# Seven block products for eight in a hybrid decoder block: Strassen's scheme in the input projections, V and O turned after it, output stages moved to the end

## The chip, the cores and the metric

The kernel runs on one core of a Trainium2 chip. Times are microseconds (us) on the device from the first to the last work of one launch. The kernel before took 1591.51 us (median of 3 runs, 1591.41 to 1595.69). The profile shows one execution of it, whose span is 1588.2 us.

The engines are named as the profile names them: PE multiplies matrices, PEld loads its stationary operand, DVE does elementwise work with one or two inputs, ACT elementwise functions with one input (copies among them), POOL is a further elementwise engine, and SP issues every DMA of this kernel, in order.

## What is computed

One decoder block, in float32, on 2048 tokens of 1024 features:

```python
xn = rms_norm(x, norm_w)
proj = xn @ w_in                       # 1024 -> 5632
u_a, z_a, q_b, f_b, i_b, og_b, z_b, g_a, g_b = jnp.split(proj, SPLIT_POINTS, axis=-1)
y_a = s5_branch(u_a, z_a, ...)         # diagonal state space, GELU, GLU (512 -> 512), SiLU gate
y_b = hgrn2_branch(q_b, f_b, i_b, og_b, z_b, lower_bounds, hgrn_norm_w)   # 4 heads of 128, gated recurrence
merged = sigmoid(g_a) * (y_a @ w_proj_a) + sigmoid(g_b) * (y_b @ w_proj_b)    # 512 -> 1024 each
return rms_norm(x + merged @ w_out, final_norm_w)                          # 1024 -> 1024
```

The input projection `xn @ w_in` is by far the largest product. It is the one that the change computes in another way.

## The kernel before

**Products in pieces.** Each float32 operand of the large products is split (`split`): ACT writes a rounded copy, the high part (L94), and DVE subtracts it from the operand, the low part (L95). A product is the sum of three matmuls: high by high, low by high, high by low. So 128 by 128 weights against 512 tokens take three matmuls of 512 columns.

**Tiles.** The tokens go in two halves of 1024 (index `a`), each of two blocks of 512 (index `b`). The 5632 columns of `w_in` are 22 slices of 256: two for u, four for a head's q and f together (QF), four for a head's values and output gates (VO), two each for the SiLU gates zb and za, four each for the merge gates ga and gb. The normalised input is prepared once per half (`norm_apply`, L191: scale, then split) into 16 pairs of tiles, which stay in SBUF.

**Slices.** `proj_feat` computes a slice with features on the partitions: per block and group of 128 features 8 steps of three matmuls (L234 to L236), 96 matmuls of 512 columns in all. The VO slices go through `proj_tok`, which puts the tokens on the partitions, since the recurrence wants V and O so: 192 matmuls of 256 columns per slice (L261 to L263). ACT takes V and O out of the accumulators (L674 to L678). So 36 slices of the first kind and 8 of the second are computed, over both halves.

**What sets the order.** PE follows the program as it is written (`manual_schedule`). The generators `weave` and `mix` put the steps of the recurrence (`hgrn_core`), of the state-space scan (`ssm`) and of the small stages between the slices. A scheduler orders the other engines by its own estimate, and each of them then works strictly in its order. A half runs from its u slices to its output: projections, merge (`merge`), output product (`out_proj`); then the second half does the same. The second half's input is normalised during the first half's output product. The merge gates wait in DRAM (`sg_d`) and the branch outputs YA and YB in SBUF.

**Buffers.** PSUM has eight banks: four for the projections (`psd`), two for the recurrence's scores (`psc`), and one each in `psm` and `pss`. Weights are loaded in pieces of 512 KB, one ahead.

Of the kernel before, what the change touches and what calls it, by code (L numbers as in the profile page):

```python
# [31 lines left out]
def hybrid_block(  # L32
# [31 lines left out]
    rp = ctx.enter_context(tc.tile_pool(name="rp", bufs=32))  # L64
    wpool = ctx.enter_context(tc.tile_pool(name="wpool", bufs=3))
    yp = ctx.enter_context(tc.tile_pool(name="yp", bufs=8))
    sp = ctx.enter_context(tc.tile_pool(name="sp", bufs=12))
# [14 lines left out]
    sg_d = [[dram.tile([128, HALF], F32, name=f"sg_d{a}_{j}") for j in range(16)] for a in range(2)]  # L82
# [3 lines left out]

    def y4(name):
        return yp.tile([128, 1024], F32, name=name, tag="y")

    def h2(name, tag):  # L90
        return hp.tile([128, 512], F32, name=name, tag=tag)

# [23 lines left out]

# [31 lines left out]
    XH = [[[None] * NBLK for _ in range(8)] for _ in range(2)]  # L148
    XL = [[[None] * NBLK for _ in range(8)] for _ in range(2)]
    rst = const.tile([128, 16], F32, name="rst")  # L150
    ssx = const.tile([128, 16], F32, name="ssx")

    def norm_stats(a, b):
        t0 = a * HALF + b * 512
        c0 = a * 8 + b * 4
        for i in range(4):
            if a == 0:
                xr = y4(f"xr{a}{b}{i}")
            else:
                xr = wpool.tile([128, 1024], F32, name=f"xr{a}{b}{i}", tag="ev", bufs=2)  # L160
# [3 lines left out]
        dg = h2(f"dg{a}{b}", "st") if a == 0 else s2(f"dg{a}{b}")  # L164
        for i in range(4):
            V.tensor_scalar(dg[:, i * 128 : (i + 1) * 128], ident, rst[:, c0 + i : c0 + i + 1], None, op0=ALU.mult)
        return dg

    rb0 = [None]

    def norm_bcast(a, b, dg):
        pool, tg = ((pss, "pss"), (psm, "psm"))[a * b]
        ps = pool.tile([128, 512], F32, name=f"psn{a}{b}", tag=tg)
        mm(ps, ones, dg, start=True, stop=True)
        rb = s2(f"rb{a}{b}")
# [3 lines left out]
    def norm_load(a, b, k):  # L179
        t0 = a * HALF + b * 512  # L180
        xr = s2(f"xtr{a}{b}{k}")
        nc.sync.dma_start(xr, xt[k, :, t0 : t0 + 512])
        return xr

    def norm_apply(a, b, rb, loaded=None, ks=range(8)):
        for k in ks:
            xr = loaded[k] if loaded else norm_load(a, b, k)
            if rb is None:
                V.tensor_scalar(xr, xr, nw_t[:, k : k + 1], None, op0=ALU.mult)
            else:  # L190
                V.scalar_tensor_tensor(xr, xr, nw_t[:, k : k + 1], rb, op0=ALU.mult, op1=ALU.mult)  # L191
            xh = rp.tile([128, 512], F32R, name=f"xh{a}{b}{k}", tag="r")
            xl = rp.tile([128, 512], F32R, name=f"xl{a}{b}{k}", tag="r")
            if a == 0 and k % 2 == 1:
                S.activation(xh, xr, AF.Copy)
                P.tensor_tensor(xl, xr, xh.bitcast(F32), op=ALU.subtract)
            else:
                split(xr, xh, xl)
            XH[a][k][b] = xh
            XL[a][k][b] = xl  # L200

    pre = {}

    def load_w(src, shape, name, parts=1):
        if name in pre:
            return pre.pop(name)
        n = shape[1] * shape[2]
        raw = wpool.tile(shape, F32, name="r" + name, tag="wr", bufs=2)
        hi = wpool.tile(shape, F32R, name="h" + name, tag="wh")
        lo = wpool.tile(shape, F32R, name="l" + name, tag="wl")  # L210
# [6 lines left out]
    def proj_feat(a, sl, evac, blks=(0, 1), defer=None, outer=False):  # L217
        ps = {}
        w = {}
        for bq in ((0,), (1,)) if outer else (blks,):  # L220
          for kh in range(2):
            if kh not in w:
                w[kh] = load_w(wi[sl, kh], [128, 4, 256], f"w{a}_{sl}_{kh}{blks[0]}", 2 if a == 0 and sl <= SL_QF else 1)
            hi, lo = w[kh]
            for ft in range(2):
                for b in bq:
                    if kh == 0:
                        ps[ft, b] = psd.tile([128, 512], F32, name=f"pd{a}_{sl}_{ft}{b}", tag="psd")
                    o = ps[ft, b]
                    for k in range(4):  # L230
# [3 lines left out]
                        mm(o, wh, XH[a][kk][b], start=(kk == 0), stop=False)  # L234
                        mm(o, wh, XL[a][kk][b], start=False, stop=False)  # L235
                        mm(o, wl, XH[a][kk][b], start=False, stop=(kk == 7))  # L236
                    if kh == 1:
                        if a == 0 and b == 0:
                            if defer is not None:
                                defer.append((evac, ft, b, o))  # L240
                                yield
                                continue
                            V.tensor_tensor(o, o, rb0[0], op=ALU.mult)
                        evac(ft, b, o)
                    yield

    def proj_tok(a, sl, evac):
        w = [load_w(wi[sl, kh], [128, 4, 256], f"w{a}_{sl}_{kh}") for kh in range(2)]
        for b in range(NBLK):
            ps = [None] * 4  # L250
            for kh in range(2):
                hi, lo = w[kh]
                for c in range(4):
                    if kh == 0:
                        ps[c] = psd.tile([128, 256], F32, name=f"pt{a}_{sl}_{b}{c}", tag="psd")
                    o = ps[c]
                    for k in range(4):
                        kk = kh * 4 + k
                        xh = XH[a][kk][b][:, c * 128 : (c + 1) * 128]
                        xl = XL[a][kk][b][:, c * 128 : (c + 1) * 128]  # L260
# [3 lines left out]
                    if kh == 1:  # L264
                        evac(b, c, o)
                    if c % 2 == 1:
                        yield

    def proj_u(a, defer=None):
        ut = {}  # L270
        for bk, ii in (((0,), (0, 1)), ((1,), (1, 0))) if a == 0 else (((0, 1), (0, 1)),):
            for i in ii:
                blks = (0, 1) if a == 0 and i == 1 else bk
                if a == 0 and i == 1 and bk == (1,):
                    continue

                def evac(ft, b, ps, i=i):
                    f = i * 2 + ft
                    if b == 0:
                        ut[f] = yp.tile([128, 8, 128], F32, name=f"ut{a}{f}", tag="y")  # L280
                    for hf in range(2):
                        src = ps[:, 0:256] if hf == 0 else ps[:, 511:255:-1]
# [966 lines left out]
```

## Time and profile before

| | |
|---|---|
| median of 3 runs | 1591.51 us |
| span of the profiled execution | 1588.2 us |
| PE busy | 1551.5 us (98%) |
| DVE busy | 944.9 us (59%) |
| ACT busy | 526.2 us (33%) |
| POOL busy | 267.6 us (17%) |
| DMA, mean share of 16 engines | 34.4% of the span on the one queue in use |

The span is what the profile covers; the measured time of a run contains a few microseconds around it. A row of the timeline gives an instruction's start, its duration, its engine, its line, the operation, and output and inputs by the program's names. Durations of matmuls overlap, since they are pipelined: what a matmul costs in a dense stream is the distance of two starts. The same holds, less strongly, for DVE and ACT.

### The profile page before, as it was taken

How to read it: one execution, taken by the hardware profiler on the slowest of the kernel's cores; microseconds unless marked ns; L12 is line 12 of the kernel's file. 1: busy time of each engine (PE TensorE's matmuls, PEld its weight loads, DVE VectorE, ACT ScalarE, POOL GpSimd, SP SyncE). 2: the span in 40 equal slices, each digit the busy share in tenths (PEclk: the TensorE clock that was granted, in tenths of full speed). 3: DMA queues.
4: the chain of work that ended last, by engine and by line, in shares of the span. 5: the costliest groups of instructions: out<-in, count | busy, mean ns of one | idle time of the engine just before them, and what ended most of it. 6: DMA issues, size and time to landing. Idle time of an engine off the chain costs nothing.

```text
span 1588.2 us, 22450 instructions
## 1 busy us (share of the span) xinstructions
PE 1551.5 (98%) x8480; PEld 1312.6 (83%) x8480; DVE 944.9 (59%) x1927; ACT 526.2 (33%) x1150; POOL 267.6 (17%) x220
## 2 busy tenths in 40 slices
PE   6999999999998999999999999999999999999997
PEld 4798888789888878888888988888887897888886
DVE  6986475567849757556252334774875447464435
ACT  5333323233333634213241322223332335341122
POOL 1100040122204022220210000212142002222120
PEclk9999999999999999999999999999999999999999
DMA  8442223523334512447152123132324210144512
GB/s 305 155 110 86 92 85 92 154 93 83 117 103 113 155 64 97 132 141 231 60 187 81 46 100 97 56 115 83 113 72 152 98 59 30 51 151 141 184 42 93
DMA packets 108284, 175.54 MB, mean 111 GB/s; under 512 B 36176, under 2 KB 52560, under 8 KB 108176
## 3 DMA queue, kind: packets, MB, share of 16 engines
q1 hardware_dynamic: 108176, 174.11, 34.4%
q8 instruction: 67, 1.10, 0.3%
q14 instruction: 41, 0.34, 0.1%
HBM read 133.43 MB, written 40.63 MB: 110 GB/s over the span
## 4 chain that ended last, share of the span: by engine, by line
PE 81%; DVE 8%; issue 6%; DMA 2%; POOL 2%; ACT 1%; SPq 0%; POOLq 0%; ACTq 0%; DVEq 0%
PE pd L234 14%; PE pd L235 14%; PE pd L236 14%; PE pf L978 4%; PE pf L977 4%; PE pf L976 4%; PE pp L939 3%; PE pp L940 3%; PE pp L938 3%; PE pt L261 3%; PE pt L262 3%; PE pt L263 3%; PE sc L738 1%; PE pv L787 1%; PE po L804 1%
## 5 line engine op out<-in xcount | busy, mean ns | idle before, releaser
L234 PE MATMUL pd<-xh,hw 128*128 128x512 f32 x1152 | 466.7, 405 | 8.2 <-ACT hw L94 7.5
L235 PE MATMUL pd<-xl,hw 128*128 128x512 f32 x1152 | 451.9, 392 | 3.2 <-DVE xl L95 2.2
L236 PE MATMUL pd<-xh,lw 128*128 128x512 f32 x1152 | 451.3, 392 | 0.1
L234 PEld LDWEIGHTS pd<-xh,hw 128*128 128x128 f32 x1152 | 217.4, 189 | 51.7 <-ACT hw L94 8.4
L236 PEld LDWEIGHTS pd<-xh,lw 128*128 128x128 f32 x1152 | 216.8, 188 | 47.3 <-DVE lw L95 0.9
L235 PEld LDWEIGHTS pd<-xl,hw 128*128 128x128 f32 x1152 | 217.4, 189 | 46.5 <-DVE xl L95 4.0
L95 DVE TENSOR_TENSOR lw<-rw,hw 128x1024 fp32r<-128x1024 f32 (+1 forms) x98 | 115.1, 1178 | 170.3 <-ACT hw L94 170.0
L94 ACT ACTIVATE hw<-rw 128x1024 fp32r<-128x1024 f32 (+1 forms) x98 | 96.1, 987 | 223.6 <-PE pd L235 142.0
L261 PE MATMUL pt<-hw,xh 128*128 128x256 f32 x512 | 146.8, 287 | 1.9 <-ACT O L678 1.9
L262 PE MATMUL pt<-lw,xh 128*128 128x256 f32 x512 | 145.6, 284 | 0.0
L263 PE MATMUL pt<-hw,xl 128*128 128x256 f32 x512 | 145.5, 284 | 0.0
L261 PEld LDWEIGHTS pt<-hw,xh 128*128 128x128 f32 x512 | 98.9, 193 | 2.9 <-ACT O L678 2.1
L262 PEld LDWEIGHTS pt<-lw,xh 128*128 128x128 f32 x512 | 99.0, 193 | 0.2
L263 PEld LDWEIGHTS pt<-hw,xl 128*128 128x128 f32 x512 | 98.9, 193 | 0.0
L594 POOL COPY T<-h 128x4 f32<-128x4 f32 x8 | 5.9, 738 | 363.3 <-DVE t L589 363.3
L775 DVE TENSOR_TENSOR Q<-Q,t 128x256 f32<-128x256 f32 x96 | 46.2, 482 | 32.5 <-PE sc L750 32.4
L904 ACT ACTIVATE sg<-pd 128x512 f32<-128x512 f32 x64 | 37.9, 593 | 82.2 <-PE pd L236 48.8
L943 POOL TENSOR_TENSOR sgl<-sgl,sgl 128x512 f32<-128x512 f32 x32 | 41.9, 1309 | 129.1 <-DVE sgl L941 95.9
L739 DVE COPY_PREDICATED s_buf<-masks,sc 128x256 f32<-128x256 uint8 x64 | 32.4, 507 | 51.5 <-PE sc L738 51.5
L733 ACT ACTIVATE KX<-K 128x128 f32<-128x128 f32 x128 | 32.6, 306 | 89.3 <-DVE K L776 73.9
L941 DVE TENSOR_TENSOR sgl<-sgl,pp 128x512 f32<-128x512 f32 x64 | 43.7, 682 | 26.9 <-PE pp L940 26.9
L939 PE MATMUL pp<-yl,hpa 128*128 128x512 f32 x128 | 50.1, 391 | 1.0 <-DVE yl L95 1.0
(326 smaller groups left out, 2811.6 us busy)
## 6 DMA issues: line engine op xcount, KB each, us to landing
rw<-in_wi_dram SPq DMA_DIRECT2D x82, 512.0 KB, 3.5
sg_d<-sg SPq DMA_DIRECT2D x32, 512.0 KB, 2.9
sgl<-sg_d SPq DMA_DIRECT2D x64, 256.0 KB, 3.0
xtr<-in_xt_dram SPq DMA_DIRECT2D x32, 256.0 KB, 6.2
xr<-in_xn_dram SPq DMA_DIRECT2D x16, 512.0 KB, 6.4
ro<-in_wo_dram SPq DMA_DIRECT2D x16, 512.0 KB, 3.9
hh<-in_xn_dram SPq DMA_DIRECT2D x32, 256.0 KB, 5.0
out_dram<-hh SPq DMA_DIRECT2D x32, 256.0 KB, 2.3
```

The costliest lines, as they stand in the source:

```text
L94: S.activation(hi, raw, AF.Copy)
L95: V.tensor_tensor(lo, raw, hi.bitcast(F32), op=ALU.subtract)
L234: mm(o, wh, XH[a][kk][b], start=(kk == 0), stop=False)
L235: mm(o, wh, XL[a][kk][b], start=False, stop=False)
L236: mm(o, wl, XH[a][kk][b], start=False, stop=(kk == 7))
L261: mm(o, xh, hi[:, k, :], start=(kk == 0), stop=False)
L262: mm(o, xh, lo[:, k, :], start=False, stop=False)
L263: mm(o, xl, hi[:, k, :], start=False, stop=(kk == 7))
L939: mm(ps, hi[:, k, fs], yl, start=False, stop=False)
L976: mm(o, mh[:, ts_], hi, start=(kk == 0), stop=False)
L977: mm(o, mh[:, ts_], lo, start=False, stop=False)
L978: mm(o, ml[:, ts_], hi, start=False, stop=(kk == 7))
```

## The change

The kernel after keeps the split into high and low parts, the two halves and PE's hand-written order. It changes the following.

- Of the first half, the two u slices and the first QF slice are still computed plainly (`proj_plain`, 96 matmuls of 512 columns each). All other slices, 19 in the first half and 22 in the second, go through `strassen`: the 2 by 2 block product (two feature halves of the weights, two halves of the input features, two token blocks) is made of 7 block products for 8, each 12 matmuls of 512 columns, 84 per slice.
- `xprep` makes the operands of the input side: for each of 4 feature pairs 4 scalings, 4 additions and 7 splits, 56 tiles per half instead of 32. The ring `y` that holds the raw input has 2 buffers.
- `w_ops` makes the 7 operands of the weight side of each slice (4 additions, 7 splits). In the first half each operand is stored to DRAM (`wc_d`, 512 KB), and the second half loads it again (19 of its 22 slices).
- Per slice three partial sums are copied out of PSUM by ACT (`snap`) and completed by DVE (`total`).
- VO slices come with features on the partitions like all others. `turn` transposes each of their four 128 by 512 results on PE (4 transposes into the bank of `psm`), and ACT copies the result out. `flush` puts the turns at the start of the next block product.
- Core steps of the heads are placed one per block product (`heads`). The branch outputs and gates go to DRAM (`ft_d`). Between the halves stand `merge_b(0)` (the HGRN branch's merge of the first half) and the second half's `xprep`. The constants of the state space (`ssm_params`, `ssm_mats`) and the scans of both halves are in the second half. GLU, the rest of the merge and the output product of both halves stand at the end.
- The tables `el_d` and `eh_d` are stored by four DMAs that write runs of 64 and 32 bytes, for two DMAs of whole rows.

```diff
+    def xprep(a, k, rbs):
+        ...
+        for b in range(2):
+            for kk, t in ((k, xa), (k + 4, xb)):
+                v = t[:, b * 512 : b * 512 + 512]
+                V.scalar_tensor_tensor(v, v, nw_t[:, kk : kk + 1], rbs[b], op0=ALU.mult, op1=ALU.mult)
+        ...
+        op(0, b11)
+        op(1, b21)
+        V.tensor_tensor(t3, b22, b12, op=ALU.subtract)
+        V.tensor_tensor(b12, b12, b11, op=ALU.subtract)
+        V.tensor_tensor(b11, b12, b22, op=ALU.subtract)
+        op(2, b11)
+        op(3, b12)
+        op(4, t3)
+        V.tensor_tensor(b21, b21, b11, op=ALU.add)
+        op(5, b21)
+        op(6, b22)
-    def proj_tok(a, sl, evac):
-        ...
-                        mm(o, xh, hi[:, k, :], start=(kk == 0), stop=False)
-                        mm(o, xh, lo[:, k, :], start=False, stop=False)
-                        mm(o, xl, hi[:, k, :], start=False, stop=(kk == 7))
+    def w_ops(a, sl):
+        ...
+        if sl in wc_d:
+            for p in range(7):
+                t = wo4(f"w{n}_{p}")
+                nc.sync.dma_start(t.bitcast(F32), wc_d[sl][p])
+                yield t
+            return
+        ...
+            split(raw, v[:, 0], v[:, 1])
+            if a == 0:
+                nc.sync.dma_start(wc_d[sl][p], t.bitcast(F32))
+        ...
+    def strassen(a, slices, ahead=2):
+        ...
+        for t, (i, p) in enumerate(order):
+            for d in range(ahead + 1):
+                fetch(t + d)
+            flush()
+        ...
+            for k in range(4):
+                xh, xl = X[a][p][k]
+                mm(o, w[:, 0, k], xh, start=(first and k == 0), stop=False, skip_group_check=True)
+                mm(o, w[:, 0, k], xl, start=False, stop=False, skip_group_check=True)
+                mm(o, w[:, 1, k], xh, start=False, stop=(k == 3), skip_group_check=True)
+        ...
+            if p == 0:
+                snap("s1")
+            elif p == 1:
+                evac(0, 0, None, total("s1", o))
+            elif p == 2:
+                snap("u2")
+            elif p == 4:
+                snap("u3")
+                evac(1, 1, None, total("u3", z[3]))
+            elif p == 5:
+                evac(1, 0, o, None)
+            elif p == 6:
+                evac(0, 1, None, total("u2", o))
+    def vo_evac(a, h):
+        ...
+            def turn():
+                o = psm.tile([128, 512], F32, name=f"pt{a}{h}{ft}{b}", tag="psm")
+                for c in range(4):
+                    nc.tensor.transpose(ch(o, c), ch(sb, c), ident)
+        ...
+            post.append(turn)
-        nc.sync.dma_start(el_d, EL.rearrange("p g r c -> p g (r c)"))
-        nc.sync.dma_start(eh_d, EH.rearrange("p g r c -> p g (r c)"))
+        nc.sync.dma_start(el_d[:, :, 0:16], ELr)
+        nc.sync.dma_start(el_d[:, :, 16:32], ELi)
+        nc.sync.dma_start(eh_d[:, :, 0:8], EH[:, 0])
+        nc.sync.dma_start(eh_d[:, :, 8:16], EH[:, 1])
```

PE, first half, end of a result of the first VO slice. Before, the slice's last matmuls, with tokens on the partitions, and what follows them:

```order
L262 MATMUL pt0_6_13_1172<-lw0_6_1_1021,xh017_482 128x256
L263 MATMUL pt0_6_13_1172<-hw0_6_1_1020,xl017_483 128x256
L234 MATMUL pd0_14_00_1247<-xh000_198,hw0_14_00_1242 128x512
L235 MATMUL pd0_14_00_1247<-xl000_199,hw0_14_00_1242 128x512
L236 MATMUL pd0_14_00_1247<-xh000_198,lw0_14_00_1243 128x512
```

After, the end of its second block product (`pd0_6_1`), the turn of the result that the product completes (`s10_6`, which DVE makes of `pd0_6_1`), and the third block product:

```order
L377 MATMUL pd0_6_1_1072<-X031h_996,w0_6_1_1039 128x512
L378 MATMUL pd0_6_1_1072<-X031l_997,w0_6_1_1039 128x512
L379 MATMUL pd0_6_1_1072<-X031h_996,w0_6_1_1039 128x512
L826 MATMUL pt0000_1090<-ident_190,s10_6_1066 128x128 x4
L377 MATMUL pd0_6_0_1053<-X002h_781,w0_6_2_1049 128x512
L378 MATMUL pd0_6_0_1053<-X002l_782,w0_6_2_1049 128x512
L379 MATMUL pd0_6_0_1053<-X002h_781,w0_6_2_1049 128x512
```

Where PE went from one slice straight to the next, four transposes now stand behind the very product that their input is made from.

DVE, at the start, the last operands of the input side in the first half. Before, scalings (`xtr`) and low parts (`xl`) of the second token block:

```order
L191 SCALAR_TENSOR_TENSOR xtr014_422<-xtr014_422,nw_t_152,rb01_432 128x512
L191 SCALAR_TENSOR_TENSOR xtr015_424<-xtr015_424,nw_t_152,rb01_432 128x512
L191 SCALAR_TENSOR_TENSOR xtr016_426<-xtr016_426,nw_t_152,rb01_432 128x512
L95 TENSOR_TENSOR xl014_468<-xtr014_422,xh014_467 128x512
L191 SCALAR_TENSOR_TENSOR xtr017_428<-xtr017_428,nw_t_152,rb01_432 128x512
L95 TENSOR_TENSOR xl016_478<-xtr016_426,xh016_477 128x512
```

After, the last feature pair (`xa03`, `xb03`; `X030l` to `X034l` are the low parts of five of its seven operands), and the sum `s10_6` that the first turn waits for:

```order
L115 TENSOR_TENSOR X030l_993<-xa03_983,X030h_992 128x512
L234 SCALAR_TENSOR_TENSOR xb03_984<-xb03_984,nw_t_200,rb00_434 128x512
...
L115 TENSOR_TENSOR X032l_1004<-xa03_983,X032h_1003 128x512
L115 TENSOR_TENSOR w0_6_2_1049<-s20_6_1044,w0_6_2_1049 128x512
L115 TENSOR_TENSOR X033l_1008<-xa03_983,X033h_1007 128x512
L115 TENSOR_TENSOR w0_6_3_1068<-s10_6_1043,w0_6_3_1068 128x512
L115 TENSOR_TENSOR X034l_1012<-t3x03_991,X034h_1011 128x512
L386 TENSOR_TENSOR s10_6_1066<-s10_6_1066,pd0_6_1_1072 128x512
```

The sum stands behind the operands of later block products; `X030l` is the 179th operation that DVE does in the program, counting repeats, and the sum is the 195th.

DVE, second half, the constants of the state space. Before, in the first half, they stand among the steps of a head and the weights of the gate slices (`lw0_15`):

```order
L95 TENSOR_TENSOR lw0_15_00_2497<-rw0_15_00_2495,hw0_15_00_2496 128x1024
L664 TENSOR_SCALAR F011_1990<-F011_1990,lbp_159 128x512
L490 TENSOR_TENSOR C3_2331<-AR_796,T1_692 128x1024
L491 TENSOR_TENSOR Tm3_2332<-AI_797,T2_693 128x1024
L495 TENSOR_TENSOR W3_2330<-AR_796,BB_887 128x1024
```

After, they stand ahead of the first weight operand of the second half's u slice (`w1_0_0`; `u21_10` and `s11_14` are totals of the slices before it):

```order
L625 TENSOR_TENSOR W3_6464<-AR_5792,BB_5893 128x1024
L652 TENSOR_TENSOR KT2_6347<-KT2_6347,dd2_6451 16x8x16
L627 TENSOR_TENSOR W3_6464<-W3_6464,Tm3_6463 128x1024
L776 SCALAR_TENSOR_TENSOR ezb110_6488<-pd1_10_0_6213,hnw_t_203,ezb110_6488 128x512
L386 TENSOR_TENSOR u21_10_6363<-u21_10_6363,pd1_10_3_6373 128x512
L776 SCALAR_TENSOR_TENSOR ezb101_6513<-u21_10_6363,hnw_t_203,ezb101_6513 128x512
L386 TENSOR_TENSOR s11_14_6438<-s11_14_6438,pd1_14_1_6529 128x512
L652 TENSOR_TENSOR KT3_6472<-KT3_6472,dd3_6578 16x8x16
L115 TENSOR_TENSOR w1_0_0_6591<-rw1_0_0_6589,w1_0_0_6591 128x512
```

The u slice is the fifth of the second half, and what DVE does from the last input operand's first split (`X130l`) to `w1_0_0` is 260 operations.

## Rows read from the trace of the kernel before

**Rows 1.** The page: span, busy time of engines, PE's granted clock over the span.

```profile
span 1588.2 us, 22450 instructions
...
PE 1551.5 (98%) x8480; PEld 1312.6 (83%) x8480; DVE 944.9 (59%) x1927; ACT 526.2 (33%) x1150; POOL 267.6 (17%) x220
...
PEclk9999999999999999999999999999999999999999
```

**Rows 2.** The chain that ended last: share of the span by engine.

```profile
PE 81%; DVE 8%; issue 6%; DMA 2%; POOL 2%; ACT 1%; SPq 0%; POOLq 0%; ACTq 0%; DVEq 0%
```

**Rows 3.** Waits of PE: who waited, for whom, us in total, times, longest.

```profile
PE pd L234 <- ACT hw L94: 7.5, 2, 6.3
PE psy L601 <- DVE T L566: 4.2, 2, 3.1
...
PE pt L261 <- ACT O L678: 1.9, 1, 1.9
```

**Rows 4.** Windows: length, busy (x starts) of PE, PEld, DVE, ACT, POOL; clock; DMA.

```profile
0.00:40.00 40.00, 27.96 (x98) 19.51 (x99) 24.48 (x60) 22.99 (x44) 7.74 (x13) 1.00 0.87 303
40.00:80.00 40.00, 38.36 (x165) 30.34 (x164) 39.78 (x169) 14.35 (x27) 7.20 (x11) 1.00 0.49 153
640.00:720.00 80.00, 80.00 (x353) 66.08 (x353) 40.88 (x53) 16.89 (x23) 19.67 (x15) 1.00 0.45 145
1520.00:1588.00 68.00, 60.03 (x265) 49.36 (x263) 34.28 (x109) 20.52 (x45) 10.71 (x8) 0.96 0.19 70
```

**Rows 5.** Groups by line and form: the projections' matmuls; DVE on PSUM; ACT's evacuation.

```profile
L234 PE MATMUL pd<-xh,hw 128*128 128x512 f32 x1152 | 466.7, 405 | 8.2 <-ACT hw L94 7.5 <-ACT xh L94 0.6
...
L261 PE MATMUL pt<-hw,xh 128*128 128x256 f32 x512 | 146.8, 287 | 1.9 <-ACT O L678 1.9
...
L941 DVE TENSOR_TENSOR sgl<-sgl,pp 128x512 f32<-128x512 f32 x64 | 43.7, 682 | 26.9 <-PE pp L940 26.9
...
L904 ACT ACTIVATE sg<-pd 128x512 f32<-128x512 f32 x64 | 37.9, 593 | 82.2 <-PE pd L236 48.8 <-DVE pd L243 16.3 <-issue 10.3
```

**Rows 6.** PE's timeline, matmuls of 256 columns: start, duration, instruction.

```profile
103.07 0.28 PE L262 MATMUL pt<-lw,xh 128*128 128x256 f32 x1
103.19 0.28 PE L263 MATMUL pt<-hw,xl 128*128 128x256 f32 x1
103.31 0.28 PE L261 MATMUL pt<-hw,xh 128*128 128x256 f32 x1
```

**Rows 7.** PE's timeline, four transposes among matmuls of 512 columns.

```profile
173.12 0.39 PE L236 MATMUL pd<-xh,lw 128*128 128x512 f32 x1
173.35 0.60 PE L760 MATMUL pk<-ident,K 128*128 128x128 f32 x4
173.71 0.48 PE L234 MATMUL pd<-xh,hw 128*128 128x512 f32 x1
174.02 0.40 PE L235 MATMUL pd<-xl,hw 128*128 128x512 f32 x1
```

**Rows 8.** DVE's timeline, back-to-back operations of 512 columns.

```profile
86.37 0.68 DVE L661 TENSOR_TENSOR Q<-Q,pd 128x512 f32<-128x512 f32 x1
86.97 0.22 DVE L296 TENSOR_TENSOR tw<-EL,ang_b 128x64 f32<-128x64 f32 x1
```

**Rows 9.** The clock around a wait of PE at 1017 us: windows, columns as in rows 4.

```profile
1017.00:1020.00 3.00, 2.42 (x17) 2.42 (x18) 1.88 (x6) 1.75 (x6) 0.71 (x1) 0.86 0.01 3
1020.00:1023.00 3.00, 3.00 (x18) 3.00 (x17) 1.23 (x1) 0.81 (x3) 0.00 (x0) 0.57 0.15 27
1023.00:1030.00 7.00, 7.00 (x50) 6.50 (x49) 2.50 (x4) 2.28 (x7) 0.00 (x0) 1.00 0.19 66
```

**Rows 10.** DMA issues: out<-in, engine, count, KB each, median us to landing.

```profile
rw<-in_wi_dram SPq DMA_DIRECT2D x82, 512.0 KB, 3.5
...
UW<-u_d SPq DMA_DIRECT2D x128, 32.0 KB, 2.3
...
E<-eh_d SPq DMA_DIRECT2D x16, 32.0 KB, 3.1
```

More of the change, by code (lines that the diff above doesn't have):

```diff
@@ L1085, in weave, with timed @@
-    def weave(dense, nd, side, ns, lead=0):
-        done = 0
-        for i in range(nd):
-            next(dense, None)
-            want = min(ns, max(0, (i + 1 - lead)) * ns // max(1, nd - lead))
-            while done < want:
-                next(side, None)
-                done += 1
-        run(dense, side)
+            next(g, None)
+    def timed(dense, n, events):
+        ev = sorted(events, key=lambda e: e[0])
+        i = 0
+        for t in range(n):
+            while i < len(ev) and ev[i][0] <= t:
+                ev[i][1]()
+                i += 1
+            next(dense, None)
+        for _, f in ev[i:]:
+            f()
@@ new lines, in heads @@
+    def heads(a, first, every=35):
+        ev = []
+        cores = [hgrn_core(a, h) for h in range(4)]
+        fins = [hgrn_fin(a, h, None if h < 3 else (lambda b, y: yb_pair(a, 3, b, y))) for h in range(4)]
+        for h in range(4):
+            t0 = first + every * h
+            for s in range(22):
+                ev.append((t0 + s, lambda c=cores[h]: step(c)))
+            ev.append((t0 + 21, lambda c=cores[h]: run(c)))
+            if h < 3:
+                for s in range(2):
+                    ev.append((t0 + 23 + 2 * s, lambda f=fins[h]: step(f)))
+        return ev, fins[3]
@@ new lines, in hybrid_block @@
+        d0 = strassen(0, slices(0))
+        ev, fin3 = heads(0, 10)
+        ev.append((60, lambda: norm_stats(1, 0)))
+        ev.append((95, lambda: norm_stats(1, 1)))
+        timed(d0, 133, ev)
+        run(d0)
+        for h in range(3):
+            for b in range(2):
+                yb_load(0, h, b)
+        rb1 = [norm_bcast(1, b) for b in range(2)]
+        mb = merge_b(0)
+        step(mb)
+        step(fin3, 2)
+        for k in range(4):
+            xprep(1, k, rb1)
+            step(mb, 4)
@@ new lines, in hybrid_block, with build @@
+        run(mb)
+        d1 = strassen(1, slices(1))
+        ev, fin3 = heads(1, 25)
+        ssm = {}
+        def build():
+            ssm["m"] = ssm_mats(*ssm_params())
+        ev.append((1, build))
+        for s in range(16):
+            ev.append((8 + s, lambda: step(ssm["m"])))
+        ev.append((24, lambda: run(ssm["m"])))
+        sg = ssm_all()
+        for b in range(8):
+            for s, d in enumerate((0, 4, 9, 13)):
+                ev.append((39 + b * 14 + d, lambda: step(sg)))
@@ L1164 @@
+        timed(d1, 154, ev)
+        run(d1, sg)
+        gl = glu()
+        step(gl, 3)
+        step(fin3)
+        step(gl)
+        step(fin3)
+        for h in range(3):
+            for b in range(2):
+                yb_load(1, h, b)
+        run(gl)
+        M = merge(0)
+        run(out_proj(0, M))
+        M = merge(1)
+        run(out_proj(1, M))
 _OUTS = [((1, L, D), "float32")]
```

956 lines of the change are left out of this document (504 added, 452 removed).

## The prediction

> **What bounds the kernel now.** I read the page first: its span, the busy time of each engine and the granted clock [rows 1]. PE is busy 1551.5 of 1588.2 us at full clock, so all its gaps together are 36.7 us, and the other engines have slack on average: DVE 59%, ACT 33%. The chain that ended last [rows 2] agrees: 81% of the span runs through PE. The waits of PE [rows 3] show few and small gaps: the largest sum is 7.5 us for a weight's high part, the longest single wait 6.3 us. Then windows [rows 4]. In the first 40 us PE is busy 27.96 us, so it loses 12.0 us at the start, and DVE itself idles 15.5 of these 40 us, waiting for its first loads and copies. The last 68 us lose 8.0 us. A steady window in the middle has 353 matmuls in 80.00 us without a gap: 0.2266 us from start to start. The kernel is a dense stream of matmuls, and a change helps if it shortens that stream and the other engines still keep ahead of it. After this change both must be counted.
>
> **What the stream loses and gains.** Three lines with 1152 matmuls of 512 columns each and three with 512 of 256 columns make the input projections [rows 5]. The small ones start 0.24 us apart in two, so 0.120 us each [rows 6]. Before: 3456 x 0.2266 + 1536 x 0.120 = 783.1 + 184.3 = 967.4 us. After: 3 plain slices of 96 and 41 slices of 7 x 12 = 84 matmuls make 3732, at 0.2266 us 845.7 us. That is 121.7 us less. The code makes exactly these counts, so I see no case in which this term fails. Against it stand 32 turns of four transposes. Four transposes between matmuls of 512 columns push the stream back [rows 7]: from 173.12 to 174.02 us lie two matmuls and the four, 0.90 - 2 x 0.227 = 0.45 us. 32 x 0.45 = 14.3 us. The stream is shorter by **107.4 us**. The other products keep their counts.
>
> **The start of the block products.** The first block product needs the first operand of all four feature pairs, the last of them `X030`. Up to its low part DVE does 179 operations, 115 of them of 512 columns. For such an operation the trace gives 0.60 us from start to start [rows 8] and a duration of 0.68 us [rows 5]; I take 0.65 us, so 74.8 us, and 11.7 us for the 64 smaller ones by their own rows' mean durations, in sum 86.5 us. DVE's 15.5 us of idle time at the start come on top, and some 5 us in which it waits for the last plain results: 107 us. PE is through the three plain slices after 288 x 0.2266 = 65.3 us and its 12.0 us of start, at 77.3 us. It waits 30 us. Before, nothing like it stands there: the slices could begin with the first block of tokens, and DVE had only 32 input tiles to make. After the first two products (5.4 us) the first turn waits for `s10_6`, 16 DVE operations or 10.3 us behind `X030l`: 4.9 us more. Less 1.6 us that PE loses between 40 and 80 us before the change [rows 4]: **+33 us**. From below 26 us (0.60 us an operation), from above 45 us (the raw input has only two buffers, so each pair also waits for its load).
>
> **Turns.** A turn stands at the start of the product behind the one that its input is made of, so PE stops while that input is made. Price of one stop from the rows: the last matmul lasts 0.39 us [rows 7] of which 0.23 are its slot, so 0.16 us; DVE's sum 0.68 us, ACT's copy 0.59 us [rows 5]. The four turns of a slice: sum 0.84; copy and sum 1.43; copy 0.75; sum 0.84; in all 3.9 us. DVE works strictly in its order and is mostly in another operation, which I charge with half of one, 0.3 us, for each of the three sums: 4.8 us a slice. Seven slices (the first is in the term above): **+33 us**. Floor 27 us, ceiling 60 us, when two or three whole operations stand ahead of each sum. Queued behind the waiting transposes is all of PE's work, block products and recurrence.
>
> **Between the halves.** The second half's input operands were made under the first half's output product. Now the only product that covers them is `merge_b(0)`, 192 matmuls or 43.5 us, and the four last steps of head 3 stand ahead of it with nothing between, through the one bank of `psm` (some 10 us). DVE does 109 operations up to `X130l`, 79 of 512 columns, 59 us. Behind it come 260 operations up to the weights of the u slice `w1_0_0` (58 of 512 columns, 24 of 1024, the rest small, by rows of the same forms 94 us), since the state space's constants stand ahead of them. PE has in the same stretch 43.5 + 1 us of merge and 4 x 84 x 0.2266 = 76.1 us of slices plus 9 us of turns and small matmuls, 129.7 us. DVE needs 59 + 94 + 10 = 163 us: **+33 us**. Floor 16 us (0.60 us an operation takes off 7, head 3's steps beside other work 10), ceiling 45 us.
>
> **Weights in the second half.** Operands are fetched two products ahead, 5.4 us, less than 1.4 us of which the stores of results ahead of them on SP take away; a 512 KB load lands in 3.5 us [rows 10]. That suffices alone. But `el_d` and `eh_d` are stored in 4 x 4096 runs of 64 or 32 bytes. Two loads of 32 KB bound a run: from `eh_d`, in 512 runs of 64 bytes, 3.1 us; from `u_d`, in 64 runs, 2.3 us [rows 10]. So 0.8 us for 448 runs, 29 us for 16384. I take half as uncovered: **+14 us**, between 0 and 50 us.
>
> By the Trainium skill (DMA: Bandwidth & Descriptors, Specifications) a transfer below 512 bytes is not at line rate and becomes a read-modify-write; the loads from `eh_d` and `u_d` [rows 10] agree in direction, but no store of such runs is in this trace. If a read-modify-write doubled a run, this term alone would be up to 58 us for 29, an estimate by that page, and it speaks against the change.
>
> **Lock-step and the end.** In the first half's 18 slices DVE has 279 us of work for 373 us of PE: 75% on average, above 80% while a head is at work, where before it is 51% in a dense window [rows 4]. PE's and DVE's waits for each other no longer vanish there; I take 0.45 us a slice, **+8 us** (0 to 30). At the end GLU waits for scans, GELU and a way through DRAM, and head 3's output for another: two chains of a 3.5 us store, a 3.5 us load and some five operations of 0.65 us, 20 us, for the 15 us that PE loses in the middle before the change (36.7, less 13.6 in the first 80 us and 8.0 at the end [rows 1, 4]): **+5 us** (-15 to 30).
>
> Sum: -107.4 + 33 + 33 + 33 + 14 + 8 + 5 = +18.6 us. The profiled span of 1588.2 us and 3.3 us around it are just the median, 1591.5 us. So 1588.2 + 18.6 + 3.3 = **1610 us**, 1.2% slower: the freed PE time goes into waits for DVE.
>
> **Rivals.** *Waits at their floor, faster.* DVE runs at 0.60 us, turns cost the bare handoff, loads are covered: start 26, turns 8 x 3.9 = 31, between the halves 20, the rest nothing: -107.4 + 77 = -30 us, 1561 us. For it: PE before never waits long for DVE although DVE is often full (4.2 us in two waits [rows 3]); against it: the two stretches in which DVE is simply longer than PE stay. *Late weights and lock-step, much slower.* SP issues in order, a load behind a store that waits for DVE comes late, and then every product of the second half pays: 50 us for 14, and 30 us for 8: 1610 + 58 = 1668 us. It decides if a load takes more than about 4 us from its issue; 3.5 us [rows 10] is near. *The clock falls in the turns.* After one wait of PE of 1.9 us [rows 3] the granted clock was 0.86 and then 0.57 for 3 us each [rows 9], so 0.14 x 3 + 0.43 x 3 = 1.7 us lost. If each of some 30 stops in the turns did so, 51 us: 1661 us. Against it: that wait came on top of other idle time of PE, and in the dense windows the clock holds.
>
> The Trainium skill (TensorE: Matmul & The Clock Gate, HAM oscillation) says that a kernel whose matmuls wait again and again falls to half clock each time and starts cold; [rows 9] show one such fall, towards the 1.2 GHz of half clock and back to full clock within six us, behind a wait.
>
> **How the numbers follow.** The forecast case 0.45, floor of the waits 0.37, late weights 0.13, clock 0.05. That the change does not do what it says I exclude: the counts are in the order. The forecast case itself spreads over 1585 to 1637 us by the bounds above. A measurement can tell 0.3%, 4.8 us, from no change; of the forecast case 0.08 fall within that and 0.01 below, of the floor case 0.01 within. Faster 0.37, within 0.09, slower 0.54. The range reaches from the floor case, a little below it, to the late weights: 1550 to 1668 us.
>
> **What would show it.** Right: a gap of PE of some 30 us before the first block product, ended by an input operand's low part (L115); waits of the transposes (L826) for the sums (L386) and copies of 0.8 to 1.5 us, about 40 us in all; another 30 us from the end of head 3 to the fifth slice of the second half, ended by DVE; PE's busy time near 1445 us. Wrong: if PE's first gap is under 20 us, DVE was faster than I count or the scheduler's order kinder; if waits for weights by DMA lead the list, the late-weights rival holds; if the clock falls below 0.9 over many slices, the last one.

## The result, and the profile after

The kernel after takes 1778.82 us (median of 4 runs, 1776.17 to 1781.56) beside 1593.6 us for the kernel before (4 runs): 1.116 times, 95% interval 1.1138 to 1.1182. It is slower, as forecast, but by 185 us and not by 18.6, and the time lies above the stated range.

The page of the changed kernel: span, busy time, granted clock and queue, the same lines as in [rows 1].

```profile
span 1775.8 us, 21543 instructions
...
PE 1510.1 (85%) x7348; PEld 1225.7 (69%) x7348; DVE 1081.0 (61%) x2226; ACT 641.4 (36%) x1361; POOL 172.2 (10%) x156
...
PEclk9879999999999897999999899798899789999999
...
q1 hardware_dynamic: 185808, 329.58, 55.3%
```

PE is idle for 265.7 us where it was idle for 36.7 [rows 1]: +229.0. It is busy for 41.4 us less, where the shorter stream should give 107.4 less: 66 us are missing. The clock shows most of these. In the changed kernel's trace PE is busy for 103.8 us at a granted clock of 0.50 (1.2 GHz, the lower of its two levels), in 23 falls, so 51.9 us are lost; before it was 1.7 us, in one fall [rows 9]. The other 16 us I have not separated. -107.4 + 229.0 + 66.0 = 187.6 us, the difference of the spans.

Windows of the changed kernel, one for each stage: start, first half's block products, from head 3's end some way into the second half, the rest of the second half's block products, GLU, output (columns as in [rows 4]).

```profile
0.00:150.00 150.00, 99.69 (x377) 76.60 (x378) 106.23 (x208) 65.84 (x123) 13.73 (x18) 0.85 0.60 190
150.00:575.00 425.00, 406.65 (x2108) 330.22 (x2107) 287.14 (x621) 206.89 (x471) 0.89 (x3) 1.00 0.67 246
575.00:800.00 225.00, 165.62 (x787) 130.88 (x785) 161.63 (x390) 65.85 (x133) 1.00 (x7) 0.86 0.53 162
800.00:1350.00 550.00, 462.30 (x2451) 380.78 (x2452) 324.77 (x661) 167.81 (x394) 66.33 (x64) 0.93 0.55 179
1350.00:1460.00 110.00, 69.58 (x284) 54.57 (x283) 62.55 (x83) 53.42 (x102) 24.73 (x16) 0.80 0.50 167
1460.00:1775.80 315.80, 306.26 (x1349) 252.64 (x1347) 138.71 (x265) 81.56 (x142) 65.50 (x48) 1.00 0.43 141
```

Idle time of PE, stage by stage: 50.3, 18.4, 59.4, 87.7, 40.4 and 9.5 us. The first half's block products are the good part: full clock, 4% idle. The second half's are not.

The waits of PE, the list that answers to [rows 3]:

```profile
PE psw L635 <- DVE W L627: 37.1, 3, 26.0
PE pg L1018 <- ACT gh L114: 31.0, 4, 13.7
PE pd L377 <- DMA w<-wc: 28.5, 5, 19.2
PE pt L826 <- DVE u L386: 18.5, 14, 2.7
PE pt L826 <- DVE s L386: 17.5, 7, 4.9
PE psn L188 <- DVE dg L185: 16.9, 1, 16.9
PE pd L377 <- ACT X030h L114: 12.6, 1, 12.6
PE psg L699 <- DMA MU<-u_d: 12.2, 1, 12.2
PE py L988 <- ACT ys L983: 11.2, 13, 3.2
PE psg L699 <- DMA U<-u_d: 9.5, 1, 9.5
...
PE pt L826 <- ACT vo L821: 4.8, 7, 0.7
```

Read from the top: transposes of the state space's weights (`psw`) wait for DVE; GLU (`pg`) waits at the end; block products of the second half wait for reloaded weights; the turns (`pt`) wait 40.8 us in three rows; `psg`, the scan's first product, waits for its loads of u. Before, the largest row had 7.5 us.

Three rows on PE's timeline show what a stop leaves behind it:

```profile
1120.58 2.05 PE L699 MATMUL psg<-MU,WV 128*128 128x128 f32 x8 [12.21 <-DMA MU<-u_d]
1126.93 0.80 PE L377 MATMUL pd<-X101h,w 128*128 128x512 f32 x1 [4.31 <-DMA w<-wc]
1127.53 0.63 PE L378 MATMUL pd<-X101l,w 128*128 128x512 f32 x1
```

The first matmul of 512 columns behind the stop lasts 0.80 us and the next 0.63, where [rows 7] have 0.39 in the dense stream. What held its weights back stands in SP's timeline ahead of it (start, duration, line, operation):

```profile
1105.69 0.43 SPq L679 DMA_DIRECT2D WV<-v_d  x1
1106.16 2.30 SPq L686 DMA_DIRECT2D MU<-u_d  x5
1116.89 0.34 SPq L760 DMA_DIRECT2D ya_d<-ya  x1
1117.28 1.73 SPq L686 DMA_DIRECT2D MU<-u_d  x3
1119.05 2.30 SPq L686 DMA_DIRECT2D U<-u_d  x5
1121.39 0.42 SPq L791 DMA_DIRECT2D sg_d<-u  x1
1121.91 0.38 SPq L302 DMA_DIRECT2D w<-wc  x1
```

SP stands from 1108.5 to 1116.9 us in front of the store of GELU's result (`ya_d`), and the scan's loads and the weights stand behind it.

### The profile page after: what moved, and what is told of

It reads as the page before. It is cut to its first block, busy times and chain, and to the rows that moved or that the text cites. A ratio compares the mean times of both kernels' runs of the same rounds, so it can differ in the third digit from the quotient of the medians.

```text
span 1775.8 us, 21543 instructions
## 1 busy us (share of the span) xinstructions
PE 1510.1 (85%) x7348; PEld 1225.7 (69%) x7348; DVE 1081.0 (61%) x2226; ACT 641.4 (36%) x1361; POOL 172.2 (10%) x156
## 5 line engine op out<-in xcount | busy, mean ns | idle before, releaser
L386 DVE TENSOR_TENSOR u<-u,pd 128x512 f32<-128x512 f32 x82 | 56.2, 686 | 110.9 <-PE pd L379 88.6
L114 ACT ACTIVATE w<-rw 128x512 fp32r<-128x512 f32 x110 | 69.0, 628 | 100.1 <-PE pd L379 54.6
L1133 PE MATMUL pf<-ho,mh 128*128 128x512 f32 x256 | 99.7, 390 | 1.7 <-DVE sgl L1102 1.7
L1134 PE MATMUL pf<-lo,mh 128*128 128x512 f32 x256 | 99.7, 390 | 0.0
L1135 PE MATMUL pf<-ho,ml 128*128 128x512 f32 x256 | 99.6, 389 | 0.0
L383 ACT ACTIVATE u<-pd 128x512 f32<-128x512 f32 x82 | 48.9, 597 | 128.9 <-PE pd L379 121.7
L115 DVE TENSOR_TENSOR w<-rw,w 128x512 fp32r<-128x512 f32 x110 | 76.7, 698 | 22.2 <-ACT w L114 21.8
L1133 PEld LDWEIGHTS pf<-ho,mh 128*128 128x128 f32 x256 | 48.0, 188 | 12.2 <-DVE sgl L1102 2.1
L1018 PE MATMUL pp<-yh,hpa 128*128 128x512 f32 x128 | 49.8, 389 | 0.0
L1020 PE MATMUL pp<-yh,lpa 128*128 128x512 f32 x128 | 49.8, 389 | 0.0
```

The lines of the kernel that those rows point to most:

```text
L114: S.activation(hi, raw, AF.Copy)
L115: V.tensor_tensor(lo, raw, hi.bitcast(F32), op=ALU.subtract)
L383: S.activation(z[key], o, AF.Copy)
L386: V.tensor_tensor(z[key], z[key], ps, op=ALU.add)
L1018: mm(ps, hi[:, k, fs], yh, start=(k == 0), stop=False)
L1020: mm(ps, lo[:, k, fs], yh, start=False, stop=(k == last))
```

## The experiments

The theory from this profile: the time is PE's shorter stream, plus stops where PE's own order meets work that another engine or queue has not finished, plus the low clock behind long stops. Rivals: the stores and reloads of weights slow everything (traffic); DVE sets the pace throughout, so that stops can only be moved; the small-run stores of the forecast.

### The turns one product later

```diff
     post = []
+    aged = []
...
     def flush():
-        for f in post[:]:
+        for f in aged:
             f()
+        aged[:] = post
         del post[:]
...
+        flush()
         flush()
```

> Each turn one block product later. Theory (stops by order): the transposes (L826) no longer wait for the sums and copies made of the product just before them; their waits, 40.8 us in the changed kernel, fall below 6 us, and the clock falls that follow the longest of them (five, some 10 us) go too: 1735 us, between 1725 and 1748. Rival (DVE is the bound): PE then waits as long at the next product for its weight operand or bank, and the time stays above 1763 us.

Measured: 1740.86 us, ratio to before 1.0933 (1.0911 to 1.0956), 38.0 us less than the changed kernel. The turns' waits are down to one row of 6.6 us:

```profile
PE pd L379 <- DMA w<-wc: 40.3, 4, 18.5
...
PE pt L829 <- DVE u L388: 6.6, 2, 5.6
```

This is the theory, and the forecast's term (33 us for seven slices, 4.9 us for the first) has the right size. The weights' waits rose by 12 us meanwhile. The loss at low clock hardly fell (48.7 us for 51.9). Of the 23 falls in the changed kernel six stand behind waits of turns (12.0 us of the loss); here one does (2.0 us), but falls behind other waits came in their place.

### Weights four ahead, GELU later

`ahead4`: `d1 = strassen(1, slices(1), 4)`. `gelu_later`: `ssm_all` issues the next batch's loads before it calls `gelu`, and calls it for the second half's tokens one batch later.

> In the second half weight operands are loaded four products ahead for two; the first half is as before. Theory (SP's queue stands still behind the GELU stores, and loads of weights stand in it): PE's waits for weight loads, 28.5 us in 5, fall below 10 us, with the clock fall of 970 us: 1753 us, between 1743 and 1765. Rival (the second half's traffic makes every load slow): the waits stay, 1772 to 1785 us. A third way: the state space's loads now stand behind weight loads that wait for PE, and its waits (21.7 us) grow: above 1785 us.

Measured: 1778.36 us (1.1167, 1.115 to 1.1183), no change. The waits for weights fell from 28.5 to 7.6 us, and the scan's loads, now queued behind more weights, took what was won (12.2 and 9.5 us in the list above):

```profile
PE psg L699 <- DMA MU<-u_d: 26.6, 2, 14.4
...
PE psg L699 <- DMA U<-u_d: 9.5, 1, 9.5
...
PE pd L377 <- DMA w<-wc: 7.6, 3, 3.0
```

This is the third way of the expectation, in a milder form.

> The next scan batch's loads are issued ahead of GELU, and GELU of the second half's tokens one batch later, so that no load waits for a buffer that GELU holds. Theory (SP's queue): PE's waits for U and MU loads, 21.7 us in 2, go, and its waits for weight loads, 28.5 us, fall to below 12 us, with three clock falls: 1738 us, between 1725 and 1752. Rival (traffic): only the two U and MU waits change, by less than half: 1765 to 1780 us.

Measured: 1768.17 us (1.1104, 1.107 to 1.1138), 10.6 us less. Both waits for u are gone and those for weights are at 7.4 us, so the queue behind GELU is what made them; but of some 43 us only a quarter came back, and the time lies in the rival's range. Waits of the heads and of GLU grew (`po` for `st` from 7.7 to 13.2, `sc` for `Q` from 1.1 to 6.9 us), and 55.6 us are lost at low clock for 51.9. The mechanism is shown; the size that I expected is not.

### Traffic and small runs

`no_wc` stores only the first of each slice's seven weight operands and reads that one seven times; `eld_rows` stores the tables in whole rows.

> Of the 133 stores of weight operands in the first half only each slice's first is left (19), and all loads of the second half read that one, so the second half's products are made with other weights; all loads stay. Rival (traffic: 58 MB of stores slow the loads and hold up SP, which waits 204 us for DVE in them): 1735 to 1760 us. Theory (SP's waits in the first half lie beside PE's work): 1768 to 1782 us.

Measured: 1788.39 us (1.1223, 1.1206 to 1.124), 9.6 us slower, not faster, and above the theory's range too. The traffic of the stores is not the cause. The reloads in the second half stayed, so of their traffic no run here says anything. PE's idle time is nearly the same (267.4 us for 265.7); 62.1 us are lost at low clock for 51.9, which is about the difference, and why the clock falls more often here stays open.

> The tables el and eh are stored in whole rows of 2 and 1 KB, as four tensors, for runs of 64 and 32 bytes. Forecast's term (these stores hold up the weight loads, 14 us): 1765 us. Theory (the late weights come from the queue behind GELU): within 4 us of the changed kernel, 1775 to 1783 us.

Measured: 1779.03 us (1.1168, 1.1151 to 1.1185), no change. The forecast's cause for late weights is refuted: in the changed kernel these stores land in 5.3 and 6.7 us, the same bytes in whole rows in 2.0 and 1.7 us (`eld_rows`), but the time does not change. Nor does it follow the loss at low clock alone: `eld_rows` loses 61.6 us for 51.9, and PE idles 259.4 us for 265.7.

```profile
el_d<-EL SPq DMA_DIRECT2D x2, 256.0 KB, 5.3
...
eh_d<-EH SPq DMA_DIRECT2D x2, 128.0 KB, 6.7
```

### The second half in another order, GLU covered

`u_first`: the slices begin with u (`s = u + [qf(0), vo(0), ...]`), the state space's transposes stand at products 17 to 31, `heads(1, 31)`. `glu_cover`: `merge_b(1)` runs ahead of `glu()`.

> In the second half the u slices come first, the state space's transposes stand at block products 17 to 31 for 8 to 24, the heads start six products later. Theory (PE's order meets work whose input DVE has not made): the three waits of psw, 37 us, fall below 12 us, with two clock falls (some 6 us): 1748 us, between 1735 and 1762. Rival (DVE's total work sets the pace of this stretch; the stop moves to another tile): 1765 to 1785 us.

Measured: 1743.37 us (1.0944, 1.0924 to 1.0964), 35.5 us less. The rows for `psw` and for GLU now read:

```profile
PE psw L635 <- DVE W L627: 17.2, 4, 10.3
...
PE pg L1018 <- ACT gh L114: 15.2, 3, 8.0
```

The waits of `psw` fell by 20 us, not below the 12 us that I expected: so much of the stop was one of order, since the same work of DVE now lies beside work of PE. The waits of GLU (`gh` and `gl`) fell by another 18 us, from 36.9 to 19.1. That I had not expected; the same edit ends the scans five block products earlier (a batch every 13 products for 14), which may be why, but it was not tried by itself. So the 35.5 us are not the price of the `psw` stop alone.

> The HGRN branch's merge of the second half (192 matmuls, 43.6 us) stands ahead of GLU and not inside the last merge. Theory (GLU's chain through DRAM and GELU has no cover): the waits of pg for gh and gl, 36.9 us, fall below 8 us, and the four clock falls from 1370 us on (some 9 us) mostly go; the merge itself may add 5 us of waits for gates: 1743 us, between 1733 and 1756. Rival (GLU's chain is longer than that cover, or head 3's chain takes its place): 1758 to 1775 us.

Measured: 1791.05 us (1.1247, 1.123 to 1.1264), 12.2 us slower and above both ranges. GLU's waits fell from 36.9 to 15.9 us, but the merge put in front stops at the same time, for its own weights, the output product waits 11.8 us for `sgl` where it waited 1.7, and the loss at low clock rises to 62.1 us:

```profile
PE pb L1018 <- ACT hpb L114: 13.3, 1, 13.3
PE pg L1018 <- ACT gh L114: 13.1, 3, 6.0
```

What is late there begins at SP. In the changed kernel PE stands from 1367.2 us on in front of GLU, and SP issues the load of GLU's weights (`rg`) only at 1370.95 us, behind stores that it waits for; ACT then waits for the load before it can split it:

```profile
1370.95 0.90 SPq L1050 DMA_DIRECT2D rg<-in_wg_dram  x2
...
1377.11 0.63 ACT L114 ACTIVATE gh<-rg 128x512 fp32r<-128x512 f32 x1 [2.35 <-DMA rg<-in_wg_dram]
```

In `glu_cover` the merge's weights (`rpb`) take the same place: issued at 1373.18 us, with PE standing from 1368.0. What ACT's own order adds behind the load is not separated.

### Who sets the pace

`thin` leaves out one matmul of twelve in each block product, `thin_before` the same in the kernel before.

> One matmul of twelve (high weight by low input of the last feature pair) is left out of every block product, so the result is less exact: 287 matmuls, 65.3 us of PE's stream. Theory now (in long stretches DVE, ACT and SP set the pace, so what PE is spared comes back as waits): 20 to 42 us faster than the changed kernel, 1737 to 1759 us. Rival (PE sets the pace between a fixed number of stops, as the forecast's sum has it): 55 to 66 us faster, 1713 to 1724 us.

> The same in the kernel before, one projection matmul of twelve left out: 288 of 512 columns and 128 of 256, 65.3 + 15.4 = 80.7 us of PE's stream. Both theories (PE sets the pace there): 1510 to 1520 us. If much more than that stays, the kernel before is not paced by PE either, and the comparison says nothing.

Measured: `thin` 1724.88 us (1.0815, 1.0785 to 1.0845), 53.9 of 65.3 us came back, 83%, just under the rival's range. PE's idle time stays at 270.3 us for 265.7, and 59.6 us are lost at low clock for 51.9. The theory written ahead of this run, that other engines set the pace in long stretches, is refuted: PE sets it, between stops whose sum hardly changes, as the forecast's sum assumed. `thin_before` 1536.2 us (0.9633, 0.9613 to 0.9653), 59.4 of 80.7 us, 74%, counted from the 1595.58 us of the kernel before beside it. That misses its expectation by 16 us; its trace has 53.0 us of idle time for 36.7 and 8.3 us lost at low clock for 1.7. By the condition set ahead of it, a comparison of the two kernels then says nothing, and the reading above rests on `thin` alone.

> The low parts of the weight operands (154 operations of 512 columns) are made by POOL for DVE. DVE is spared some 100 us, nearly all in the first half, where POOL is nearly idle; one such operation takes POOL about 1.3 us for 0.65. Theory (DVE's order makes the stops at the start and in the turns of the first half, DVE's load sets the lock-step): 1750 to 1768 us. Rival (POOL's longer operation makes weights late, or slows DVE): 1780 to 1800 us.

Measured: 1818.82 us (1.14, 1.138 to 1.142), 40 us slower and above both ranges, with `P.tensor_tensor(v[:, 1], raw, ...)` for DVE's subtraction. One such operation takes POOL 1376 ns, and DVE's own operations get longer; one of their rows in the changed kernel, then here:

```profile
L319 POOL TENSOR_TENSOR w<-rw,w 128x512 fp32r<-128x512 f32 x110 | 151.1, 1376 | 453.9 <-ACT w L318 253.0 <-DMA rw<-in_wi_dram 121.9 <-DVE s L387 21.1
...
L929 DVE TENSOR_TENSOR K<-K,t 128x256 f32<-128x256 f32 x96 | 43.8, 456 | 0.3
...
L930 DVE TENSOR_TENSOR K<-K,t 128x256 f32<-128x256 f32 x96 | 61.1, 637 | 1.1 <-ACT KX L887 0.2
```

Of these 96 operations the 34 that run beside one of POOL's subtractions last 958 ns on the mean, the other 62 last 461. So DVE was hardly spared: 154 operations went to POOL, and DVE is busy for 1065.4 us where it was 1081.0. The waits of turns for `s` rise from 17.5 to 28.9 us, and the loss at low clock from 51.9 to 71.9 us. This is the rival, in a worse form; what less work for DVE would bring, the run does not say.

### What a stop costs

`clock_fill` puts matmuls that nobody reads in front of seven waits (here the first of them):

```diff
+    def fill(n, x, pool, tg):
+        ps = pool.tile([128, 512], F32, name=f"fill{fills[0]}", tag=tg)
+        ...
+            mm(ps, ones_r, x, start=True, stop=True, skip_group_check=True)
...
+        fill(65, PX[0][0][0], psm, "psm")
         rb0[1] = norm_bcast(0, 1)
```

> Matmuls that nobody reads (272 of 512 columns, 62 us at full clock) are put in front of seven waits: 65 ahead of the wait for the second block's norm (16.9 us in the changed kernel), 50 inside the first block product (12.6 us), 95 ahead of the first transposes of the state space's weights (26 us), 50, 38, 12 and 12 ahead of GLU's four waits. Nothing else changes. Theory (the clock falls in a stop and PE pays behind it): PE's idle time shrinks by the fill, its clock stays up at these places, and of the 52 us lost at low clock some 20 go: 1762 us, between 1755 and 1769. Rival (the lower clock behind a stop costs nothing, since other engines set the pace there): 1775 to 1785 us.

Measured: 1779.37 us (1.1169, 1.1151 to 1.1188), no change. The clock is higher in the three stages with fills, as its windows show beside those above (0.95 for 0.85, 0.90 for 0.86, 0.92 for 0.80):

```profile
0.00:150.00 150.00, 125.41 (x499) 97.47 (x499) 105.68 (x210) 67.13 (x125) 14.38 (x18) 0.95 0.59 194
575.00:800.00 225.00, 191.25 (x885) 151.78 (x884) 163.77 (x393) 67.10 (x134) 0.98 (x7) 0.90 0.53 165
1350.00:1460.00 110.00, 88.44 (x373) 69.43 (x372) 60.64 (x81) 52.48 (x100) 23.28 (x16) 0.92 0.47 163
```

But PE only reached the next wait earlier: the first turn starts at 132.6 us (133.4 in the changed kernel), the first `psw` at 709.7 (711.4). Over the whole kernel the loss fell by 3.6 us only, to 48.3, since falls came elsewhere and 4.2 us of it lie in the fills themselves. The first of GLU's fills also stands behind a wait and not in front of it, since it reads the weights that PE waits for (the row below), and GLU's first product comes 9.5 us later than in the changed kernel:

```profile
PE fill L176 <- ACT gh L114: 10.9, 1, 10.9
```

So the run does not say what the clock costs where PE has a clear way ahead. For that, 16 stops of three lengths went into the kernel before, one behind each gate slice: a transpose, ACT's copy of it, 0, 2 or 4 operations of POOL, and a transpose that waits for them.

```diff
+        nc.tensor.transpose(ps, ident, ident)
+        S.activation(t[:, 0:128], ps, AF.Copy)
+        for _ in range(4):
+            P.tensor_tensor(t, t, t, op=ALU.mult)
+        nc.tensor.transpose(ps, t[:, 0:128], ident)
```

> The kernel before, with 16 added stops of PE, one behind each gate slice: PE transposes a constant, ACT copies the result, PE transposes the copy. One stop should last about 0.8 us (drain and ACT's copy). If a stop costs its length: 13 us and some 5 us for the added instructions, 1604 to 1614 us. No clock fall is expected.

> The same with two POOL operations of 512 columns in the chain, about 1.3 us each: stops of some 3.5 us. Length alone: 16 x 2.6 = 42 us above the one without POOL. If each also makes the clock fall, as behind the stop of 1.9 us in the kernel before, 1.7 us more each: 69 us above it.

> The same with four POOL operations: stops of some 6 us. Length alone: 84 us above the one without POOL. With a clock fall behind each of 1.7 to 3 us: 111 to 132 us above it, and 27 to 48 us lost at low clock in its trace. If the time behind a stop at low clock is made up by waits that PE would have had anyway, the time is nearer to 84.

| | time, us | above before | PE's waits at the 16 stops | lost at low clock |
|---|---|---|---|---|
| before | 1594.66 | | | 1.7 |
| `stop0` | 1629.82 | 35.2 | 18.0 | 10.6 |
| `stop2` | 1698.42 | 103.8 | 66.2 | 37.5 |
| `stop4` | 1740.87 | 146.2 | 107.0 | 39.8 |

Ratios to before: 1.0214 (1.0196 to 1.0232), 1.0649 (1.0632 to 1.0667), 1.0922 (1.0901 to 1.0943). Behind one of the longer stops:

```profile
462.55 0.48 PE L916 MATMUL pb<-ident,tb 128*128 128x128 f32 x1 [7.57 <-POOL tb L915]
462.67 0.78 PE L234 MATMUL pd<-xh,hw 128*128 128x512 f32 x1
463.25 0.63 PE L235 MATMUL pd<-xl,hw 128*128 128x512 f32 x1
463.67 0.63 PE L236 MATMUL pd<-xh,lw 128*128 128x512 f32 x1
464.10 0.63 PE L234 MATMUL pd<-xh,hw 128*128 128x512 f32 x1
```

Matmuls start 0.43 us apart behind it, for 0.227 in the dense stream. `stop2` is 68.6 us above `stop0`, as the expectation with clock falls has it (69); the waits explain 48.2 and the low clock 26.9. `stop4` is 111.0 above it, at the lower end of 111 to 132, by 89.0 and 29.2. Length alone falls short both times, length and clock together are 6 and 7 us too much; between the profiled executions themselves, which differ by 72.5 and 115.2 us, they are 3 us too much. Of the 16 added stops 15 in `stop2` and all in `stop4` have a clock fall behind them, with 31.4 and 32.2 us lost; the rest of the losses in the table lies behind other waits. So in this dense stream a stop of 4.1 or 6.7 us on the mean costs its length and 2.0 us at the low clock. `stop0` missed its expectation (1604 to 1614 us): its stops last 1.1 us for 0.8, two of them have a fall behind them (3.2 us), falls behind other waits lose the rest, and some 9 us are neither wait nor clock.

By the Trainium skill (TensorE: Matmul & The Clock Gate, HAM oscillation) a kernel whose matmuls wait again and again pays for a falling clock each time; `stop2` and `stop4` agree, with 19 and 20 intervals at a granted clock of 0.50 in their traces for 2 in the kernel before.

### Together

> Together: turns one product later, u slices first with the later transposes, GELU after the next batch's loads, weights four products ahead in the second half, and at the start the second block's input loaded ahead of the statistics. If the stops add up (38 + 35 + 11 us measured singly, and 20 to 30 us of weight waits and of the start, which showed nothing singly): 1665 to 1690 us. If stops come back elsewhere: 1700 to 1735 us.

`comb2` is the turns later, u first, GELU later, weights four ahead, and the second block's input loaded ahead of its statistics: 1694.0 us (1.0619, 1.0602 to 1.0636), 84.8 us less than the changed kernel. The first three measured 84.1 us singly, so the sum is what they would give by adding up, with nothing from the other two; the range for that case, which counted on 20 to 30 us from them, ends 4 us lower. At the start its PE waits 11.0 us for the norm and 18.0 for input operands, 29.0 in all, for 16.9 + 4.4 + 12.6 = 33.9 in the changed kernel: moved, hardly removed. PE idles 182.9 us for 265.7, but 56.1 us are lost at low clock, in 24 falls for 23. No version with the change beats the kernel before, and 98 us of the difference stay.

## Why the prediction was wrong

Its direction and its frame held: the stream is shorter by the counts, PE sets the pace between stops (`thin`), and the stops' sum decides. Its sizes did not. By its terms:

- *Start*, +33: measured +36.6 us of idle time (50.3 less 13.7). Right in sum, by luck: 16.9 us of it is the wait for the second block's norm, which I did not see, and PE is done with what it could do before only at 102.5 us, not at 77.3. DVE makes `X030l` at 121.8 us and not at 107. The two errors nearly cancel: the waits for `X020` and `X030` are 4.4 and 12.6 us and not 30.
- *Turns*, +33: right, 40.8 us of waits with the first slice's 4.9, and 38 us came back when they were moved.
- *Between the halves*, +33: 59.4 us of idle time in that stage. I charged DVE's work against PE's as two totals. But PE's order puts the transposes `psw` at the eighth product, long before DVE's total is done, so PE stops there 37.1 us although it has slices to do; `u_first` takes 20 us of these waits away.
- *Weights in the second half*, +14: 28.5 us for weights and 21.7 for u, 50.2 us, and not by small runs (`eld_rows`): SP waits in front of GELU's store. I had this queue only in a rival, at 50 us. As PE's idle time the term is 36 us too small, but taking most of it away (`gelu_later`) gave 10.6 us.
- *Lock-step*, +8: 18.4 us idle in the first half's block products, but 13.3 of them are its turns; some 5 us are left for this term.
- *The end*, 20 us gross: 40.4.
- *The clock*, 0: 51.9 us lost. This is the step that failed most. The sum took each stop at its length, and the clock stood in a rival of 0.05 that put it into the turns. The price of that rival, 1.7 us a stop, was near the 2.0 measured in `stop2` and `stop4` and the 2.3 a fall here; the place was wrong for the most part: six of 23 falls, 12.0 us, stand behind turns, the other 17 behind other stops.

PE's busy time came out at 1510.1 us where the forecast's sign was 1445.

Of the 169 us between forecast and measurement, by PE's idle time and clock in the trace, the three terms that were too small make 26 + 36 + 20 = 82 us and the clock 50. The rest is PE's unseparated 16 us and some 20 us of small waits (`py` for `ys`, `po`) and of the terms that were nearly right. And the range failed because late weights and falling clock were alternatives in it, each against a sum that was otherwise right; they came together: four of the 23 falls stand behind waits for weights or u. That is what the trace adds up to; by experiment 84.8 us of the 185 were taken off (`comb2`), and the clock's price was shown in the kernel before, not in the changed one.

What stays open: how much of the 52 us at low clock the changed kernel could get back (nothing at the start and at `psw`, where another wait follows), what the reloads' traffic costs, and how much of the stop before GLU is ACT's order and how much SP's.

## What to carry to other kernels

Where PE's order is written by hand, compare for each product that needs another engine's work the point where PE gets there with the point where that work is done; totals over a stage hide stops. Look in each in-order DMA queue for a store that waits for a long chain of elementwise work, and name what stands behind it. Charge a stop in a dense stream of matmuls with its length and with the low clock behind it (here 2.0 us for stops of 4.1 and 6.7 us on the mean, and a fall behind two of 16 stops of 1.1 us); and let the terms of a bad case add up in the range, since one stop feeds the next.

## What was not expected of the hardware

A stop of 4.1 us costs PE as much clock as one of 6.7 (31.4 and 32.2 us lost behind 16 of them), with matmuls 0.43 us apart behind it. Keeping the clock up with idle matmuls (272 of them) left the time as it was, and where the next wait was for the same late engine, at the start and at `psw`, PE only waited there. And DVE slows beside POOL: the same operation of 256 columns took 958 ns beside POOL's subtractions and 461 without them (`pool_w`).
